# A two-block model on one core: where weight slabs are split around a sublayer change, and in which halves the second token tile is transposed

## The chip, the cores and the metric

The program runs on one core of one Trainium2 chip, as one launch. The metric is device microseconds of an execution, from the first to the last instruction of the core and the little that lies around it. Before the change three runs gave 1186.57, 1189.31 and 1192.03 us; the median is 1189.31 us.

## The reference

Two networks run one behind the other on a sequence of 256 tokens and a model width of 1024, all in float32.

```python
# first block: DEPTH = 2 layers
h = h + merge_heads(mix) @ w_o[layer]                 # MoBA attention, then forgetting attention
h = h + squared_relu_mlp(rms_norm(h, mlp_norm[layer]), w_up[layer], w_down[layer])   # D_FF = 4096
...
return rms_norm(h, final_norm)

# second block: nine vectors sh, sc, g from a condition c
h = modulate(rmsnorm(x, norm_ffn1[l]), sh1, sc1)
x = x + 0.5 * g1[:, None, :] * swiglu(h, ffn1_w_gate[l], ffn1_w_up[l], ffn1_w_down[l])   # width 2816
h = modulate(rmsnorm(x, norm_mix[l]), sh2, sc2)
x = x + g2[:, None, :] * hybrid_mixer(h, ...)         # state space and latent attention
h = modulate(rmsnorm(x, norm_ffn2[l]), sh3, sc3)
x = x + 0.5 * g3[:, None, :] * swiglu(h, ffn2_w_gate[l], ffn2_w_up[l], ffn2_w_down[l])
return rmsnorm(x, norm_final)
```

`swiglu(h)` is `(silu(h @ w_gate) * (h @ w_up)) @ w_down`. Here the second MLP of the first block is called M1, the first SwiGLU F1, the hybrid mixer X, and the second SwiGLU F2. The change touches the three borders M1 to F1, F1 to X, and X to F2.

## The kernel before, in words

Every product is made of three matmuls in a fast format: each operand is split into a high part and a low part, and high·high, high·low and low·high are added up in PSUM. The splits are the main work of the other engines. For a weight slab (256 rows by 512 columns, 512 KB) one DMA on SP's queue fills a tile `raw`; ScalarE (ACT) casts it into `wh` (line 179, or 183 with a gain), and VectorE (DVE) subtracts to get `wl` (line 180 or 184). There are five buffers for `raw` and five for `wh` and `wl` together, so a load is issued when the slab five places earlier has been split.

The tokens are two tiles, `t` = 0 and 1, of 128 tokens each. The normalised activations are transposed by TensorE (PE, line 272, four 128x128 transposes for a half of the 1024 features), cast by ACT into `xh` (line 266) and split by DVE into `xl` (line 267). These transposed tiles `xT` have four buffers of the kind "x".

A list `plan` holds all slabs in the order in which they are loaded and split. `take(i)` gives the product that needs slab `i` its parts, and it also splits up to two later slabs ahead, in the order of the list. Loads of the modulation weights (`w_ada`) are mixed into the list; four of them end in a cross-partition sum on POOL (line 509). Two kinds of slabs do not use the five buffers: *early* slabs, the first 768 rows of the next sublayer's first weight, have buffers of their own (`qh`, `ql`, lines 169 and 170); *spare* slabs, the second column half of the last but one down product, use the "x" buffers of the `xT` that the last up product reads, so they can only be split when that product is through with them.

A sublayer with a hidden layer goes cut by cut: the up product (F1 and F2: gate and up products) of cut j, then the down product of cut j-1. The up products take weights as the stationary side and 256 tokens as columns (lines 252 to 254); the down products and the first products of a sublayer take token blocks as the stationary side (lines 219 to 221, 512 columns). In the list, the early slabs of the next sublayer stand behind the last up product, just ahead of the last down slabs (`following`, in `plan_hidden`).

At the end of a sublayer the order is by token tile: column halves 0 and 1 of tile 0, then the spare half's products for tile 1, then tile 1. Each finished piece is added to `h` by DVE and starts a piece of the next norm. Such side chains are Python generators that a counter advances between products (`tick`, `yield n`), and `finish` runs one to its end. The normed tile goes through `modulated`, which writes `hn` (line 1029) and then transposes both halves. For tile 1, `finish(chains[1])` ahead of tile 1's first product runs both halves in one go, so PE gets eight transposes, ACT two casts and DVE two splits in a row; behind them come the splits of the next weight slabs.

Engines run their instructions in order. The order is that of the written program; nothing reschedules it.

Of the kernel before, what the change touches and what calls it, by code (L numbers as in the profile page):

```python
# [28 lines left out]
def kernel(ctx: ExitStack, tc: tile.TileContext, a: dict, out: bass.AP):  # L29
# [42 lines left out]
    def tok(t):  # L72
        return slice(t * TP, (t + 1) * TP)
# [42 lines left out]
    hold = []  # L116
    midway, second = [], []
    on_pool = set()

# [71 lines left out]
    def take(i):  # L191

        load_ahead()
        more = 0 if hold else 2 if i else 1
        while at["prep"] < len(plan):
            e = plan[at["prep"]]
            if at["prep"] > i:
                own = e[0] is not None and (e[6] or e[7])
                if not more or not (own or at["live"] < WB):
                    break  # L200
                more -= e[0] is not None and not own
            prepare()
            load_ahead()
        return ready[i]
# [206 lines left out]
    def plan_hidden(ups, w_down, cuts, rate, after=0, ahead=None, following=None):  # L411

        up, down = [], []
        for j in range(len(cuts) + 1):
            mixed["rate"] = rate if after < j < len(cuts) - 1 else 0.0
            if j < len(cuts):
                c0, n = cuts[j]
                got = [slab(w, 0, 8, c0, n, g, m=2 if n == 512 else 4) if j + i or not ahead else
                       ahead + slab(w, 6 * TP, 2, c0, n, g) for i, (w, g) in enumerate(ups)]
                up.append(got)  # L420
            if j == len(cuts) and following is not None:
                following()
            if j > 0:
                c0, n = cuts[j - 1]
                down.append([slab(w_down, c0, n // TP, s * 512, 512,
                                  spare=following is not None and j == len(cuts) - 1 and s == 1) for s in range(2)])
        mixed.update(rate=0.0, due=0.0)
        return up, down
# [413 lines left out]
    def hidden(plans, cuts, up, update, order=None, tail=None):  # L842
# [5 lines left out]
        for j in range(len(cuts) + 1):  # L848
            new = up(j, ups[j]) if j < len(cuts) else None
            if j == 1:  # L850
                acc = [[acc_ps() for _ in range(2)] for _ in range(2)]
# [173 lines left out]

    def modulated(xT, t, src, ys, r, shift):

        for s in range(2):
            DVE.scalar_tensor_tensor(out=ys[s], in0=src[s], scalar=r, in1=shift[:, cols(s)], op0=OP.mult, op1=OP.add)

        yield 8 if t else 4
        into_xT(xT, t, 0, blocks(ys[0]))
        yield 1
        into_xT(xT, t, 1, blocks(ys[1]))

# [5 lines left out]
    def norm_chain(shift, gain):  # L1041

        xT, ss, ys, chains = [], [None, None], [[], []], [None, None]

        def part(t, s):
# [6 lines left out]
            if s == 1:  # L1052
                yield 1
                r = rsqrt(total(ss[t], 2, EPS))
                yield from modulated(xT, t, ys[t], ys[t], r, shift)

# [4 lines left out]
    def two_norms_chain(fin, shift, gain):  # L1061

        xT, ss, su, u, chains = [], [None, None], [None, None], [[], []], [None, None]

        def part(t, s):
# [8 lines left out]
            if s == 1:  # L1074
# [5 lines left out]
                rr, r = rsqrt(w), rsqrt(v)  # L1080
                yield from modulated(xT, t, halves(h[t]), [sb("rb", name="hn") for _ in range(2)], rr, shift)
                start(residual(t, r))
# [10 lines left out]
    def ready_tokens(chains):  # L1093

        def before(t, k):
            finish(chains[t])
            if t == 1:
                hold.clear()
        return before

# [76 lines left out]
    def mixer(xT, chains, gate, next_chain, between):  # L1177
# [304 lines left out]
        acc = [[acc_ps() for _ in range(2)] for _ in range(2)]  # L1482
        finish(*norms)
        for n in range(3):
            if n == 1:
# [166 lines left out]
```

## Time and profile before

| what | value |
|---|---|
| median of 3 runs | 1189.31 us (1186.57 to 1192.03) |
| profiled execution, its own time | 1188.71 us |
| its span, first to last instruction | 1187.0 us |
| mean granted clock of TensorE | 0.996 of full speed |
| PE busy | 1162.7 us, 98% of the span |
| DVE busy | 832.5 us, 70% |
| ACT busy | 673.9 us, 57% |
| POOL busy | 250.8 us, 21% |
| DMA | 243.04 MB, mean 205 GB/s |

The profiled execution lies 0.6 us under the median of the three runs. The span is cut into 40 slices on the page: PE is at nine tenths or more in nearly all of them. Matmuls are pipelined, so one is shown as 0.39 us long while the next starts 0.23 us behind it; the pace is read from start to start. An idle time in brackets at the end of a row is what the engine waited just before that instruction, and behind the arrow stands what ended the wait. M1 ends and F1 begins near 600 us of the span, F1 ends and X begins near 800 us, X ends and F2 begins near 995 us.

### The profile page before, as it was taken

What the parts mean: (1) busy time and instruction counts of PE and PEld (TensorE: products, weight loads), DVE (VectorE), ACT (ScalarE), POOL (GpSimd) and SP (SyncE); (2) the same over time, 40 slices, a digit from 0 to 9 for tenths busy, and PEclk for the clock granted to TensorE, in tenths of its full rate; (3) what the DMA queues carried; (4) which work ended last, traced back from release to release, by engine and by line L of the source; (5) the groups of instructions that cost most, each with busy time, mean ns of one, the idle gap of its engine ahead of it and who ended that gap; (6) DMA issues with size and microseconds to landing.
All of it is one profiled execution on the core that took longest, in us unless ns stands there. A gap on an engine that the chain in (4) does not pass through costs nothing. (4 is left out here: it accounts for less than half of the span.)

```text
span 1187.0 us, 19943 instructions
## 1 busy us (share of the span) xinstructions
PE 1162.7 (98%) x7669; PEld 1047.6 (88%) x7669; DVE 832.5 (70%) x1187; ACT 673.9 (57%) x1148; POOL 250.8 (21%) x226
## 2 busy tenths in 40 slices
PE   8999999999999999999999999999998999999997
PEld 7987989988898799899878999978987887999996
DVE  5664678886666467788687788766776786766445
ACT  6476675565556675566654444535766573444443
POOL 3044202223003502112002121103147400112001
PEclk9999999999999999999999999999999999999999
DMA  8643567887553348799737978843733273777661
GB/s 270 195 142 107 181 219 262 295 287 223 170 174 123 129 151 282 242 308 318 244 133 256 314 274 303 275 154 101 222 92 107 90 268 125 244 222 246 209 193 38
DMA packets 128479, 243.04 MB, mean 205 GB/s; under 512 B 8515, under 2 KB 16612, under 8 KB 128384
## 3 DMA queue, kind: packets, MB, share of 16 engines
q1 hardware_dynamic: 126688, 239.96, 61.4%
q0 software_dynamic: 1376, 1.28, 0.5%
q8 instruction: 60, 0.98, 0.3%
q10 hardware_dynamic: 320, 0.53, 0.1%
q14 instruction: 35, 0.29, 0.1%
HBM read 240.65 MB, written 1.09 MB: 204 GB/s over the span
## 5 line engine op out<-in xcount | busy, mean ns | idle before, releaser
L179 ACT CAST wh<-raw 128x1024 fp32r<-128x1024 f32 (+1 forms) x231 | 237.4, 1041 | 220.3 <-DMA raw<-in_w_down_dram 64.1
L180 DVE TENSOR_TENSOR wl<-raw,wh 128x1024 fp32r<-128x1024 f32 (+1 forms) x201 | 261.5, 1319 | 128.0 <-ACT wh L179 125.9
L252 PE MATMUL mm<-xh,wh 128*128 128x256 f32 x1088 | 308.5, 284 | 0.0
L254 PE MATMUL mm<-xh,wl 128*128 128x256 f32 x1088 | 307.9, 283 | 0.0
L253 PE MATMUL mm<-xl,wh 128*128 128x256 f32 x1088 | 307.9, 283 | 0.0
L184 DVE SCALAR_TENSOR_TENSOR wl<-raw,cols,wh 128x512 fp32r<-128x512 f32 (+1 forms) x270 | 203.8, 806 | 65.2 <-ACT wh L183 65.1
L219 PE MATMUL acc<-wh,mh 128*128 128x512 f32 x524 | 208.0, 397 | 2.4 <-ACT mh L266 2.4
L183 ACT ACTIVATE wh<-raw,cols 128x512 fp32r<-128x512 f32 (+1 forms) x270 | 176.0, 708 | 59.3 <-PE acc L253 20.1
L253 PEld LDWEIGHTS mm<-xl,wh 128*128 128x128 f32 x1088 | 208.8, 192 | 0.8
L252 PEld LDWEIGHTS mm<-xh,wh 128*128 128x128 f32 x1088 | 208.8, 192 | 0.8
L254 PEld LDWEIGHTS mm<-xh,wl 128*128 128x128 f32 x1088 | 208.7, 192 | 0.0
L221 PE MATMUL acc<-wh,ml 128*128 128x512 f32 x524 | 205.1, 391 | 0.0
L220 PE MATMUL acc<-wl,mh 128*128 128x512 f32 x524 | 204.9, 391 | 0.0
L509 POOL PARTITION_ALL_REDUCE ada<-ada x18 | 64.3, 3572 | 338.2 <-DVE ada L504 140.2
L219 PEld LDWEIGHTS acc<-wh,mh 128*128 128x128 f32 x524 | 98.9, 189 | 24.4 <-ACT mh L266 4.0
L221 PEld LDWEIGHTS acc<-wh,ml 128*128 128x128 f32 x524 | 98.6, 188 | 22.5 <-DVE ml L267 1.5
L220 PEld LDWEIGHTS acc<-wl,mh 128*128 128x128 f32 x524 | 99.0, 189 | 19.1 <-DVE wl L180 0.5
L504 DVE SCALAR_TENSOR_TENSOR ada<-raw,c_act,ada 128x512 f32<-128x512 f32 x144 | 107.8, 748 | 3.5 <-DMA raw<-in_w_ada_dram 1.0
L252 PE MATMUL acc<-xh,wh 128*128 128x256 f32 x352 | 102.0, 290 | 0.0
L253 PE MATMUL acc<-xl,wh 128*128 128x256 f32 x352 | 99.5, 283 | 0.0
L254 PE MATMUL acc<-xh,wl 128*128 128x256 f32 x352 | 99.5, 283 | 0.0
L180 POOL TENSOR_TENSOR wl<-raw,wh 128x1024 fp32r<-128x1024 f32 x30 | 71.8, 2396 | 108.9 <-ACT wh L179 103.7
(320 smaller groups left out, 1602.4 us busy)
## 6 DMA issues: line engine op xcount, KB each, us to landing
raw<-in_w_ada_dram SPq DMA_DIRECT2D x72, 512.0 KB, 5.4
raw<-in_w_up_dram SPq DMA_DIRECT2D x64, 512.0 KB, 4.8
raw<-in_w_down_dram SPq DMA_DIRECT2D x64, 512.0 KB, 5.6
raw<-in_ffn_w_gate_dram SPq DMA_DIRECT2D x44, 512.0 KB, 4.9
raw<-in_ffn_w_up_dram SPq DMA_DIRECT2D x44, 512.0 KB, 4.8
raw<-in_ffn_w_down_dram SPq DMA_DIRECT2D x44, 512.0 KB, 4.8
raw<-in_moba_w_qkv_dram SPq DMA_DIRECT2D x23, 512.0 KB, 5.8
raw<-in_w_in_dram SPq DMA_DIRECT2D x20, 512.0 KB, 4.4
```

The costliest lines, as they stand in the source:

```text
L179: ACT.copy(hi, raw)
L180: (POOL if i in on_pool else DVE).tensor_tensor(lo, raw, f(hi), op=OP.subtract)
L183: ACT.mul(hi[:, k], raw[:, k], gain[k])
L184: DVE.scalar_tensor_tensor(out=lo[:, k], in0=raw[:, k], scalar=gain[k], in1=f(hi[:, k]), op0=OP.mult, op1=OP.subtract)
L219: PE.matmul(p, lhsT=xh, rhs=wh, start=first and n == 0, stop=False)
L220: PE.matmul(p, lhsT=xh, rhs=wl, start=False, stop=False)
L221: PE.matmul(p, lhsT=xl, rhs=wh, start=False, stop=last and n == len(ws) - 1)
L252: PE.matmul(o, lhsT=wh[:, c], rhs=xh, start=k == 0 and n % 2 == 0, stop=False)
L253: PE.matmul(o, lhsT=wh[:, c], rhs=xl, start=False, stop=False)
L254: PE.matmul(o, lhsT=wl[:, c], rhs=xh, start=False, stop=k == 7 and n % 2 == 1)
L504: DVE.scalar_tensor_tensor(out=acc, in0=raw[:, i, :], scalar=c_act[:, k:k + 1], in1=acc, op0=OP.mult, op1=OP.add)
L509: POOL.partition_all_reduce(acc, acc, TP, ReduceOp.add)
```

## The change

Three things change. In `plan_hidden`, the early slabs of the next sublayer now stand ahead of the last up product's slabs instead of behind it. `take` no longer splits a spare slab ahead of time before `spare["free"]` is set, which happens once the last up product and its hidden part have been written. In `modulated`, tile 1's halves become two chains that `ready_tokens` finishes one by one, the second only ahead of the fifth block of 128 features; tile 0's second half is split into its cast and, one `tick` later, its subtraction. `k // 4` is 0 for the first four blocks of 128 features and 1 for the rest.

```diff
--- before.py
+++ after.py
@@ -115,6 +115,7 @@
     mixed = {"rate": 0.0, "due": 0.0}
     hold = []
     midway, second = [], []
+    spare = {"free": False}
     on_pool = set()
 
     def slab(w, r0, nk, c0, n, gain=None, m=None, early=0, spare=False):
@@ -196,7 +197,7 @@
             e = plan[at["prep"]]
             if at["prep"] > i:
                 own = e[0] is not None and (e[6] or e[7])
-                if not more or not (own or at["live"] < WB):
+                if not more or not (own or at["live"] < WB) or (e[0] is not None and e[7] and not spare["free"]):
                     break
                 more -= e[0] is not None and not own
             prepare()
@@ -413,13 +414,13 @@
         up, down = [], []
         for j in range(len(cuts) + 1):
             mixed["rate"] = rate if after < j < len(cuts) - 1 else 0.0
+            if j == len(cuts) - 1 and following is not None:
+                following()
             if j < len(cuts):
                 c0, n = cuts[j]
                 got = [slab(w, 0, 8, c0, n, g, m=2 if n == 512 else 4) if j + i or not ahead else
                        ahead + slab(w, 6 * TP, 2, c0, n, g) for i, (w, g) in enumerate(ups)]
                 up.append(got)
-            if j == len(cuts) and following is not None:
-                following()
             if j > 0:
                 c0, n = cuts[j - 1]
                 down.append([slab(w_down, c0, n // TP, s * 512, 512,
@@ -847,6 +848,8 @@
         ups, downs = plans
         for j in range(len(cuts) + 1):
             new = up(j, ups[j]) if j < len(cuts) else None
+
+            spare["free"] = j == len(cuts) - 1
             if j == 1:
                 acc = [[acc_ps() for _ in range(2)] for _ in range(2)]
             if 0 < j < len(cuts):
@@ -1023,15 +1026,28 @@
         ACT.activation(out=a_bc, in_=a_bc, func=AF.Exp)
 
 
-    def modulated(xT, t, src, ys, r, shift):
+    def modulated(xT, t, src, ys, r, shift, parts):
 
         for s in range(2):
             DVE.scalar_tensor_tensor(out=ys[s], in0=src[s], scalar=r, in1=shift[:, cols(s)], op0=OP.mult, op1=OP.add)
-
-        yield 8 if t else 4
-        into_xT(xT, t, 0, blocks(ys[0]))
-        yield 1
-        into_xT(xT, t, 1, blocks(ys[1]))
+        if t == 0:
+            yield 4
+            into_xT(xT, t, 0, blocks(ys[0]))
+            yield 1
+
+            hi, lo = (x[:, :, tok(t)] for x in xT[1])
+            p = mm_ps((TP, 4, TP))
+            for j, b in enumerate(blocks(ys[1])):
+                PE.transpose(p[:, j, :], b, ident)
+            ACT.copy(hi, p)
+            yield 1
+            DVE.tensor_tensor(lo, p, f(hi), op=OP.subtract)
+            return
+
+        def half(s):
+            yield 1000
+            into_xT(xT, t, s, blocks(ys[s]))
+        parts += [start(half(s)) for s in range(2)]
 
     def add_gated(acc, t, c, gate):
         y = sb("ra", (TP, c.stop - c.start), name="gated")
@@ -1040,7 +1056,7 @@
 
     def norm_chain(shift, gain):
 
-        xT, ss, ys, chains = [], [None, None], [[], []], [None, None]
+        xT, ss, ys, chains = [], [None, None], [[], []], [None, None, []]
 
         def part(t, s):
             if s == 0:
@@ -1052,7 +1068,7 @@
             if s == 1:
                 yield 1
                 r = rsqrt(total(ss[t], 2, EPS))
-                yield from modulated(xT, t, ys[t], ys[t], r, shift)
+                yield from modulated(xT, t, ys[t], ys[t], r, shift, chains[2])
 
         def go(t, s):
             chains[t] = start(part(t, s))
@@ -1060,7 +1076,7 @@
 
     def two_norms_chain(fin, shift, gain):
 
-        xT, ss, su, u, chains = [], [None, None], [None, None], [[], []], [None, None]
+        xT, ss, su, u, chains = [], [None, None], [None, None], [[], []], [None, None, []]
 
         def part(t, s):
             if s == 0:
@@ -1078,7 +1094,8 @@
                 DVE.tensor_tensor(w, su[t][:, 0:1], su[t][:, 1:2], op=OP.add)
                 DVE.scalar_tensor_tensor(out=w, in0=v, scalar=EPS, in1=w, op0=OP.mult, op1=OP.add)
                 rr, r = rsqrt(w), rsqrt(v)
-                yield from modulated(xT, t, halves(h[t]), [sb("rb", name="hn") for _ in range(2)], rr, shift)
+                yield from modulated(xT, t, halves(h[t]), [sb("rb", name="hn") for _ in range(2)], rr, shift,
+                                     chains[2])
                 start(residual(t, r))
 
         def residual(t, r):
@@ -1096,6 +1113,8 @@
             finish(chains[t])
             if t == 1:
                 hold.clear()
+
+                finish(chains[2][k // 4])
         return before
 
     def ffn(plans, xT, chains, gate, next_chain, between, tail=None):
@@ -1481,6 +1500,7 @@
 
         acc = [[acc_ps() for _ in range(2)] for _ in range(2)]
         finish(*norms)
+        spare["free"] = True
         for n in range(3):
             if n == 1:
                 between()
```

The first place is DVE's order around the last gate product of F1. Before:

```order
L1150 TENSOR_TENSOR gu<-sg,mm 128x512
L267 TENSOR_TENSOR ml<-gu,mh 128x512
L1150 TENSOR_TENSOR gu<-sg,mm 128x512
L267 TENSOR_TENSOR ml<-gu,mh 128x512
L504 SCALAR_TENSOR_TENSOR ada<-raw,c_act,ada 128x512 x2
L180 TENSOR_TENSOR wl<-raw,wh 128x1024 x12
L170 TENSOR_TENSOR ql<-raw,qh 128x400 x6
L180 TENSOR_TENSOR wl<-raw,wh 128x1024 x2
L1150 TENSOR_TENSOR gu<-sg,mm 128x512
L267 TENSOR_TENSOR ml<-gu,mh 128x512
L1150 TENSOR_TENSOR gu<-sg,mm 128x512
L267 TENSOR_TENSOR ml<-gu,mh 128x512
```

Now (line 170 has become 171, 180 has become 181, 1150 is 1169):

```order
L1169 TENSOR_TENSOR gu<-sg,mm 128x512
L268 TENSOR_TENSOR ml<-gu,mh 128x512
L1169 TENSOR_TENSOR gu<-sg,mm 128x512
L268 TENSOR_TENSOR ml<-gu,mh 128x512
L505 SCALAR_TENSOR_TENSOR ada<-raw,c_act,ada 128x512 x2
L171 TENSOR_TENSOR ql<-raw,qh 128x400 x6
L181 TENSOR_TENSOR wl<-raw,wh 128x1024 x10
L1169 TENSOR_TENSOR gu<-sg,mm 128x512
L268 TENSOR_TENSOR ml<-gu,mh 128x512
L1169 TENSOR_TENSOR gu<-sg,mm 128x512
L268 TENSOR_TENSOR ml<-gu,mh 128x512
```

`ql` is the low part of an early slab of X, `ada` a step of the modulation, `wl` the low part of a weight slab. The six `ql` have moved from behind twelve `wl` to ahead of the first; the first `wl` of the row of ten belongs to the first slab of the last gate product. Six `wl` (two of them spare) now stand behind the hidden part (`gu`, `ml`) where two stood.

The second place is ACT's order at the same kind of border in M1, around the last up product. Before:

```order
L179 CAST wh<-raw 128x1024 x4
L886 ACTIVATE relu<-mm 128x512
L888 ACTIVATE sq<-relu 128x512
L266 CAST mh<-sq 128x512
L886 ACTIVATE relu<-mm 128x512
L888 ACTIVATE sq<-relu 128x512
L266 CAST mh<-sq 128x512
L183 ACTIVATE wh<-raw,cols_122 128x512 x8
L179 CAST wh<-raw 128x1024 x4
L169 CAST qh<-raw 128x512 x6
L179 CAST wh<-raw 128x1024 x2
```

Now (line 169 has become 170, 183 has become 184, 266 is 267, 886 is 889):

```order
L180 CAST wh<-raw 128x1024 x4
L170 CAST qh<-raw 128x512 x6
L889 ACTIVATE relu<-mm 128x512
L891 ACTIVATE sq<-relu 128x512
L267 CAST mh<-sq 128x512
L889 ACTIVATE relu<-mm 128x512
L891 ACTIVATE sq<-relu 128x512
L267 CAST mh<-sq 128x512
L184 ACTIVATE wh<-raw,cols_122 128x512 x8
L180 CAST wh<-raw 128x1024 x2
```

`qh` is the high part of an early slab of F1; `relu`, `sq` and `mh` evacuate an up product, and the eight `wh` with `cols` are the slabs of the last up product. The six `qh` now stand ahead of the evacuation of the last but one up product, and two of four plain `wh` have moved away behind the next evacuation.

The third place is DVE's order when M1 gives over to F1. Before:

```order
L267 TENSOR_TENSOR xl<-mm,xh 128x4x128 x2
L893 SCALAR_TENSOR_TENSOR h_103<-acc,r_5017,h_103 128x512
L1069 TENSOR_TENSOR u<-h_103,fin 128x512
L1073 TENSOR_TENSOR h_103<-u,mod 128x512
L1087 TENSOR_SCALAR h_102<-u,y 128x512 x2
L1077 TENSOR_SCALAR v<-ss 128x1
L1078 TENSOR_TENSOR w<-su 128x1
L1079 SCALAR_TENSOR_TENSOR w<-v,w 128x1
L1029 SCALAR_TENSOR_TENSOR hn<-h_103,y,mod 128x512 x2
L267 TENSOR_TENSOR xl<-mm,xh 128x4x128 x2
L180 TENSOR_TENSOR wl<-raw,wh 128x1024 x4
```

Now (line 893 has become 896 and stands just ahead of the first row shown, 1087 is 1104, 1029 is 1032):

```order
L1044 TENSOR_TENSOR xl<-mm,xh 128x4x128
L1085 TENSOR_TENSOR u<-h_103,fin 128x512
L1089 TENSOR_TENSOR h_103<-u,mod 128x512
L1093 TENSOR_SCALAR v<-ss 128x1
L1094 TENSOR_TENSOR w<-su 128x1
L1095 SCALAR_TENSOR_TENSOR w<-v,w 128x1
L1032 SCALAR_TENSOR_TENSOR hn<-h_103,y,mod 128x512 x2
L1104 TENSOR_SCALAR h_102<-u,y 128x512 x2
L1104 TENSOR_SCALAR h_103<-u,y 128x512 x2
L268 TENSOR_TENSOR xl<-mm,xh 128x4x128
L181 TENSOR_TENSOR wl<-raw,wh 128x1024 x4
L268 TENSOR_TENSOR xl<-mm,xh 128x4x128
```

Line 893 is the last sum of tile 1 into `h`, `hn` the modulated norm, line 1087 a scaling of the residual that only the end of F1 reads. The last sum now stands ahead of the second `xl` of tile 0. Of tile 1's two `xl`, the first now stands behind four scalings, of which two stood ahead of the norm and two behind the `wl` before, and the second stands behind the four `wl`. At the other two borders it is the same without the scalings. ACT has the same order there: one `xh`, four `wh`, one `xh`.

## Rows read from the trace of the kernel before

**Rows 1.** The page, busy time of each engine, share of the span, instructions.
```profile
PE 1162.7 (98%) x7669; PEld 1047.6 (88%) x7669; DVE 832.5 (70%) x1187; ACT 673.9 (57%) x1148; POOL 250.8 (21%) x226
```

**Rows 2.** Waits of PE, whole span: us in total, times, longest us.
```profile
PE acc L219 <- ACT mh L266: 2.4, 2, 1.6
...
PE mm L272 <- DVE hn L1029: 1.4, 2, 1.1
```

**Rows 3.** Timeline of PE, ends of M1 and F1: start us, us, instruction, idle before.
```profile
591.50 0.39 PE L221 MATMUL acc<-wh,ml 128*128 128x512 f32 x1
...
597.00 0.39 PE L221 MATMUL acc<-wh,ml 128*128 128x512 f32 x1
...
605.86 0.39 PE L221 MATMUL acc<-wh,ml 128*128 128x512 f32 x1
...
783.48 0.39 PE L221 MATMUL acc<-wh,ml 128*128 128x512 f32 x1
...
790.86 0.40 PE L221 MATMUL acc<-wh,ml 128*128 128x512 f32 x1
```

**Rows 4.** Stretches: length, busy time by engine, granted clock (PEclk), DMA share, GB/s.
```profile
787.20:790.60 3.40, 3.40 (x8) 2.44 (x8) 2.89 (x3) 2.88 (x4) 0.00 (x0) 0.50 0.09 31
811.10:814.50 3.40, 3.40 (x11) 3.40 (x11) 3.01 (x5) 1.79 (x4) 0.00 (x0) 0.50 0.33 84
```

**Rows 5.** Timeline of ACT, end of F1.
```profile
775.59 1.05 ACT L179 CAST wh<-raw 128x1024 fp32r<-128x1024 f32 x1 [4.71 <-PE mm L253]
...
781.89 1.05 ACT L179 CAST wh<-raw 128x1024 fp32r<-128x1024 f32 x1 [1.72 <-DMA raw<-in_ffn_w_down_dram]
```

**Rows 6.** Timelines of DVE, POOL and PE around F1's last gate product.
```profile
750.24 1.22 DVE L180 TENSOR_TENSOR wl<-raw,wh 128x1024 fp32r<-128x1024 f32 x1
751.38 3.26 DVE L180 TENSOR_TENSOR wl<-raw,wh 128x1024 fp32r<-128x1024 f32 x1
...
777.82 3.00 DVE L170 TENSOR_TENSOR ql<-raw,qh 128x400 fp32r<-128x400 f32 x6
...
750.51 4.05 POOL L509 PARTITION_ALL_REDUCE ada<-ada  x1 [19.97 <-ACT wh L179]
...
752.48 0.28 PE L252 MATMUL mm<-xh,wh 128*128 128x256 f32 x1
```

**Rows 7.** Timelines of SP, ACT, DVE and PE around M1's last up product.
```profile
561.62 1.53 SPq L149 DMA_DIRECT2D raw<-in_w_up_dram  x2
...
563.53 0.59 ACT L886 ACTIVATE relu<-mm 128x512 f32<-128x512 f32 x1
...
567.90 5.39 DVE L184 SCALAR_TENSOR_TENSOR wl<-raw,cols,wh 128x512 fp32r<-128x512 f32 x8
...
572.03 0.28 PE L252 MATMUL mm<-xh,wh 128*128 128x256 f32 x1
```

**Rows 8.** Chain that ended last: a load at F1's end by itself.
```profile
777.93 3.89 DMA raw<-in_ffn_w_down_dram
```

**Rows 9.** DMA issues from 543 to 587 us: count, size, median us to landing.
```profile
raw<-in_w_down_dram SPq DMA_DIRECT2D x10, 512.0 KB, 5.8
```

**Rows 10.** Timeline of DVE, M1 giving over to F1.
```profile
611.99 0.88 DVE L1087 TENSOR_SCALAR h<-u,y 128x512 f32<-128x512 f32 x2
...
613.91 1.42 DVE L1029 SCALAR_TENSOR_TENSOR hn<-h,y,mod 128x512 f32<-128x512 f32 x2 [0.66 <-POOL y L324]
616.10 1.35 DVE L267 TENSOR_TENSOR xl<-mm,xh 128x512 fp32r<-128x512 f32 x2 [0.77 <-ACT xh L266]
617.70 4.63 DVE L180 TENSOR_TENSOR wl<-raw,wh 128x1024 fp32r<-128x1024 f32 x4 [0.26 <-ACT wh L179]
```

**Rows 11.** Timelines of DVE and PE, F1 giving over to X.
```profile
803.07 0.69 DVE L267 TENSOR_TENSOR xl<-mm,xh 128x512 fp32r<-128x512 f32 x1 [0.81 <-ACT xh L266]
...
811.36 2.76 DVE L180 TENSOR_TENSOR wl<-raw,wh 128x576 fp32r<-128x576 f32 x4
...
810.17 0.45 PE L219 MATMUL acc<-qh,xh 128*128 128x400 f32 x1 [1.00 <-ACT xh L266]
```

## The prediction

> **What bounds the kernel now.** I read the busy times first: PE is busy for 98% of the span, and the next engine, DVE, for 70% [rows 1]. So a gain can only come out of PE's few gaps, and each new gap is paid in full. The waits of PE come second. Those that this change can reach are two waits for the hidden part's cast, 2.4 us together, the longer 1.6, and two for tile 1's normed halves, 1.4 us [rows 2]. Third comes the timeline, for what a gap costs beyond its own length. In the quiet stretch at M1's end 39 matmuls of 512 columns start in 8.86 us, 0.227 us each. Fifteen starts at the end of M1 take 5.50 us where 15 x 0.227 = 3.41 would do, so 2.1 us are lost; at the end of F1 fifteen take 7.38, so 4.0 are lost [rows 3]. The rest of the 4.0 is the clock: 3.4 us at half of it, the lower of its two levels, follow F1's gap, and 3.4 us more follow the gaps at F1's border with X [rows 4]. A fall of the clock thus costs 3.4/2 = 1.7 us. Fourth, what ends the gap at F1's end: ACT's cast of the second spare slab stands in line until the last matmul of the up product has read `xT` (4.71 us of waiting, to 775.59), and the load that the five full buffers held back arrives at 781.89 [rows 5]. The hidden part stands behind both.
>
> **The change part by part.** The sum is made against the profiled execution's own 1188.71 us.
>
> *Ends of M1 and F1, a gain.* With the early slabs done and the spare splits behind the hidden part, nothing stands between the last up product and `mh`. In F1 the evacuation takes about 3 us after the product, and PE has 24 x 0.227 = 5.4 us of down products before it needs anything new. The last down loads sit in the buffers by then, because the early slabs gave theirs back. DVE then makes one split per 1.16 us (a quarter of 4.63 [rows 10]), while PE uses one per 6 matmuls or 1.36 us at the tightest place. I take both losses as gone: -2.1 and -4.0. Bounds: at the least half of each, if one split is late; no more than all.
>
> *F1's last gate product, a loss.* What the early slabs left behind they now meet here: six `ql` on DVE stand ahead of the first `wl` of that product. Before, this `wl` began at 750.24 and ended at 751.46, and the product began at 752.48; its third matmul, 0.24 later at 752.72, is the first that needs `wl` [rows 6]. The cover is 1.3 us. The six `ql` take 3.00 us. And the same place has the cross-partition sum on POOL, from 750.51 on: the split that met it took 3.26 us where the one ahead of it took 1.22, so 2.04 more [rows 6]. Either a `ql` or the `wl` meets it now. So the `wl` ends at 750.24 + 3.00 + 2.04 + 1.22 = 756.5, and PE waits 3.8 us. That gap is longer than the 1.6 us that preceded a fall of the clock, so I add 1.7: +5.5. Bounds: +1.7 (3.00 less the 1.3 of cover, no stretch, no fall) and +6.5 (one more `wl` late).
>
> The Trainium skill, page "SBUF — State Buffer", section "Who interferes with whom", says that a DVE instruction with two SBUF inputs contends with a GpSimd instruction that reads SBUF, and that the one that comes first keeps the shared ports for its whole length. The stretched `wl` has two such inputs, and so have all six `ql`. The trace agrees on the stretch, 3.26 beside 1.22. By the rule as it stands a `ql` would wait for the whole 3.2 us that a sum lasts once it has the ports, not for 2.04, and the term would be +6.7; I keep the row's number.
>
> *M1's last up product, a small loss.* Here the `qh` stand on ACT ahead of the evacuation of the product before. They take over SP's issue places of the first three up slabs; the third of these is 561.62 + 1.16 = 562.78 [rows 7]. A load by itself lands after 3.89 us [rows 8], at 566.7; two casts of half a slab (0.53 each, half of 1.05 [rows 5]) end at 567.7. The `relu` that began at 563.53 begins 4.2 us later. The first split of the up product ended at 567.90 + 0.67 (an eighth of 5.39) = 568.57 and now ends at 572.8; PE needs it two matmuls after 572.03, at 572.3 [rows 7]. So +0.5. Bounds: 0, and +2.4 if the load takes the 5.8 us that loads take on this busy queue [rows 9].
>
> *Tile 1 of the three borders, a loss twice.* Before, both `xl` of tile 1 were made ahead of four weight splits. Now PE has 12 matmuls with the first half, then the transposes of the second, and that half's `xl` stands behind four `wl`. From the first `xl` to the second DVE needs 4.63 + 0.68 = 5.3 us [rows 10]; PE has, after the two matmuls that need no `xl`, 10 x 0.227, four transposes at about 0.35, and two matmuls more, 3.1 in all. It waits 2.2, and the second transposes, which a wait covered before, show for 0.35: +2.6. This holds for M1 to F1 and for X to F2. At M1 to F1 the last sum comes 0.68 earlier (half of 1.35), so `hn`, which ended at 615.33, ends at 614.65; but four scalings at 0.44 now stand ahead of the first `xl`, which begins at 616.4 where it began at 616.10 [rows 10]: +0.3. So +2.9 and +2.6. Bounds for each: +1 (ACT and DVE half hidden) and +4.6 with a fall of the clock.
>
> *F1 to X.* The last sum stood behind an `xl` that waited 0.81 us and took 0.69; it is 1.5 us earlier, and so is the product that began at 810.17 [rows 11]. Its weights are narrower: four `wl` take 2.76, with the `xl` 3.4 us, against 12 x 0.18 (400 of 512 columns of 0.227) + 0.35 = 2.5 of PE's, so 0.9 of waiting and 0.35 of transposes come in. That is -0.2 with the fall of the clock after 811 kept [rows 4], and -1.9 without it. I take -1.2, nearer to the second, as the gaps become shorter.
>
> *Nothing for the rest.* The number of loads, splits, matmuls and transposes is the same; POOL's order does not change.
>
> **Sum.** -2.1 - 4.0 + 5.5 + 0.5 + 2.9 + 2.6 - 1.2 = +4.2 us, so 1192.9 us against the profiled execution. That one lies 0.6 under the median of its three runs; I put 1193.2.
>
> **The rivals.**
>
> *A. The clock falls at the new gaps of tile 1 too.* M1 to F1 and X to F2 get gaps of about 1 us on either side of two matmuls. For it: at F1 to X two waits of 1.1 and 1.0 us with eight transposes between them preceded a fall [rows 2, 4, 11]. Against it: M1's end had a wait of 0.8 (2.4 less 1.6) and no fall [rows 2]. Each fall adds 1.7: one gives 1194.9, both 1196.6, which is slower by 0.6%. It decides when PE stands still about as long in sum as at F1 to X.
>
> *B. Only the gains come.* If DVE reaches the six `ql` before the hidden part keeps it busy, and the second `xl` are ready in time, only -2.1 - 4.0 - 1.9 is left: 1180.7. For it speaks that DVE has 30% free over the span [rows 1]. Against it speaks the order on DVE and ACT, which they cannot leave; it needs the splits to run twice as fast as their rows.
>
> *C. The sum on POOL keeps DVE out for its whole length,* as the rule of the skill has it: +1.2 on the gate term, 1194.4. For it: the sum's 4.05 us [rows 6]. Against it: the split's 3.26 in the same rows.
>
> **How the numbers follow.** About 0.5%, 5.9 us, is what a measurement of this kernel can tell from no change: slower begins at 1195.3, faster ends at 1183.4. My forecast, that gains and new waits nearly cancel, gets 0.58; its own terms are good to some 2.5 us, so I give 0.46 to no change and 0.12 to slower. A gets 0.26: 0.10 of it within, 0.16 slower. B gets 0.08, of which 0.07 faster and 0.01 within. C gets 0.08: 0.05 within, 0.03 slower. That makes 0.07 faster, 0.62 the same, 0.31 slower. The range runs from 1187.0 (gate term at its lower bound, the rest as summed, less 2 us of spread of the runs) to 1198.5 (A with both falls and 2 us more). What is left out is B and the upper ends of several terms together.
>
> **What the profile of the changed kernel would show.** PE's waits for `mh` at the ends of M1 and F1 gone, and no half clock after F1's up product. A wait of PE for a `wl` of some 3.8 us at the start of F1's last gate product, DVE's six `ql` just ahead of it with one of them or the first `wl` stretched to 2.5 us or more, and half clock behind. Waits of PE for `xh` and `xl` of 2 us in the middle of tile 1's first product, at M1 to F1 and X to F2, with four `wl` on DVE right ahead of that `xl`. ACT's `relu` of M1's last but one up product some 4 us later against PE. I am wrong if the gate product starts without a wait, if tile 1's second half is split in time, or if the time falls under 1187.

## The result and the profile after

The changed kernel takes 1196.60 us (median of 4 runs, 1195.45 to 1200.87), the kernel before 1187.94 beside it (median of 4, 1186.30 to 1192.03): a ratio of 1.0082, 95% interval 1.0064 to 1.0099. It is slower by 0.8%. The range held the time, but the likeliest case, no change that can be measured, did not come. The profiled execution took 1195.72 us with a span of 1194.0, against 1188.71 and 1187.0, so the two traces differ by 7.0 us and show most of the 8.7 of the medians.

I compared when the same matmul starts in both traces, stage by stage: each step of that difference is a gain or a loss in its place.

| place | predicted | trace |
|---|---|---|
| M1's last up product | +0.5 | +0.9 |
| M1's end | -2.1 | -2.1 |
| M1 to F1 | +2.9 | +3.1 |
| F1's last gate product | +5.5 | +5.8 |
| F1's end | -4.0 | -4.0 |
| F1 to X | -1.2 | +0.4 |
| X to F2 | +2.6 | +3.2 |

That is +7.3, less 0.3 of drift ahead of the first of these places. PE's own work is the same; its waits are others.

The page's busy times, which answer to [rows 1], and below them PE's waits over the whole span, which answer to [rows 2]:

```profile
PE 1162.9 (97%) x7669; PEld 1048.9 (88%) x7669; DVE 831.3 (70%) x1187; ACT 673.8 (56%) x1148; POOL 248.6 (21%) x226
```

```profile
PE mm L255 <- DVE wl L181: 4.1, 1, 4.1
PE mm L220 <- ACT xh L267: 3.5, 5, 0.8
PE acc L220 <- ACT xh L267: 3.5, 4, 1.6
PE mm L222 <- DVE xl L268: 2.1, 2, 1.1
```

The two waits for `mh` are gone, and one of 4.1 us for a weight split stands at the top, followed by tile 1's `xh` and `xl`. The timeline of PE at the ends of M1 and F1 answers to [rows 3]:

```profile
592.11 0.39 PE L222 MATMUL acc<-wh,ml 128*128 128x512 f32 x1
...
595.51 0.39 PE L222 MATMUL acc<-wh,ml 128*128 128x512 f32 x1
...
604.35 0.39 PE L222 MATMUL acc<-wh,ml 128*128 128x512 f32 x1
...
790.88 0.39 PE L222 MATMUL acc<-wh,ml 128*128 128x512 f32 x1
...
794.28 0.39 PE L222 MATMUL acc<-wh,ml 128*128 128x512 f32 x1
```

Fifteen starts take 3.40 us at both ends, where they took 5.50 and 7.38. ACT shows why at F1's end [rows 5]: the casts of `mh` come first now, and the spare slabs' casts behind them, with no load to wait for.

```profile
783.12 0.62 ACT L267 CAST mh<-gu 128x512 fp32r<-128x512 f32 x1 [7.54 <-DVE gu L1169]
785.10 0.62 ACT L267 CAST mh<-gu 128x512 fp32r<-128x512 f32 x1 [1.35 <-DVE gu L1169]
785.62 4.85 ACT L180 CAST wh<-raw 128x1024 fp32r<-128x1024 f32 x5
```

F1's last gate product (DVE, POOL, PE) answers to [rows 6]:

```profile
752.30 5.04 DVE L171 TENSOR_TENSOR ql<-raw,qh 128x400 fp32r<-128x400 f32 x6
...
752.79 2.61 DVE L171 TENSOR_TENSOR ql<-raw,qh 128x400 fp32r<-128x400 f32 x1
...
757.26 2.35 DVE L181 TENSOR_TENSOR wl<-raw,wh 128x1024 fp32r<-128x1024 f32 x2
752.57 3.40 POOL L510 PARTITION_ALL_REDUCE ada<-ada  x1 [19.41 <-ACT qh L170]
754.05 0.28 PE L253 MATMUL mm<-xh,wh 128*128 128x256 f32 x1
758.53 0.39 PE L255 MATMUL mm<-xh,wl 128*128 128x256 f32 x1 [4.09 <-DVE wl L181]
```

The six `ql` (the first row) take 5.04, which is 3.00 and the 2.04 that the sum on POOL adds; the first `wl` starts only then. The whole stretch lies on the second of the six (the row of 2.61); the other five take 0.56 to 0.57 each. The stretches at half clock (length, busy time by engine, granted clock) answer to [rows 4]; the last two are tile 1's at the borders into F1 and F2:

```profile
758.90:762.30 3.40, 3.40 (x19) 3.40 (x18) 2.49 (x3) 2.42 (x3) 0.00 (x0) 0.51 1.02 375
813.30:816.70 3.40, 3.40 (x14) 3.25 (x12) 2.23 (x4) 1.13 (x2) 0.00 (x0) 0.51 0.59 180
613.50:622.10 8.60, 6.09 (x27) 4.12 (x26) 7.36 (x10) 5.45 (x7) 0.00 (x0) 1.00 0.41 126
1000.80:1009.50 8.70, 6.16 (x28) 4.14 (x27) 5.92 (x6) 5.45 (x7) 0.00 (x0) 1.00 0.43 129
```

The fall after F1's up product is gone, one behind the gate product has come, and the one at F1 to X has stayed. M1's last up product (ACT, DVE, PE) answers to [rows 7]: `relu` starts at 567.57 instead of 563.53, and PE waits 0.28 for the first split.

```profile
567.57 0.59 ACT L889 ACTIVATE relu<-mm 128x512 f32<-128x512 f32 x1
571.94 5.39 DVE L185 SCALAR_TENSOR_TENSOR wl<-raw,cols,wh 128x512 fp32r<-128x512 f32 x8
572.75 0.39 PE L255 MATMUL mm<-xh,wl 128*128 128x256 f32 x1 [0.28 <-DVE wl L185]
```

M1 giving over to F1, DVE and then PE, answers to [rows 10]:

```profile
614.94 0.68 DVE L268 TENSOR_TENSOR xl<-mm,xh 128x512 fp32r<-128x512 f32 x1
615.81 4.63 DVE L181 TENSOR_TENSOR wl<-raw,wh 128x1024 fp32r<-128x1024 f32 x4 [0.19 <-ACT wh L180]
620.36 0.69 DVE L268 TENSOR_TENSOR xl<-mm,xh 128x512 fp32r<-128x512 f32 x1
614.89 0.50 PE L220 MATMUL mm<-qh,xh 128*128 128x512 f32 x1 [0.78 <-ACT xh L267]
618.10 0.60 PE L273 MATMUL mm<-ident,hn 128*128 128x128 f32 x4
619.38 0.50 PE L220 MATMUL mm<-qh,xh 128*128 128x512 f32 x1 [0.68 <-ACT xh L267]
621.10 0.50 PE L222 MATMUL mm<-qh,xl 128*128 128x512 f32 x1 [0.99 <-DVE xl L268]
```

The second `xl` stands 4.63 us behind, as forecast, and PE stops at tile 1's first product, in its middle for `xh` and once more for `xl`. F1 giving over to X, PE, then ACT, then one row of DVE, answers to [rows 11]:

```profile
809.96 0.60 PE L273 MATMUL mm<-ident,hn 128*128 128x128 f32 x4
812.19 0.45 PE L220 MATMUL acc<-qh,xh 128*128 128x400 f32 x1 [1.64 <-ACT xh L267]
816.03 0.99 PE L273 MATMUL mm<-ident,hn 128*128 128x128 f32 x4
817.69 0.45 PE L220 MATMUL acc<-qh,xh 128*128 128x400 f32 x1 [0.67 <-ACT xh L267]
810.54 0.48 ACT L1239 COPY cq<-acc 128x384 f32<-128x384 f32 x1 [2.76 <-DVE dtr L1237]
811.05 0.52 ACT L306 ACTIVATE junk<-cq 128x384 f32<-128x384 f32 x1
811.57 0.56 ACT L267 CAST xh<-mm 128x512 fp32r<-128x512 f32 x1
...
817.66 0.69 DVE L268 TENSOR_TENSOR xl<-mm,xh 128x512 fp32r<-128x512 f32 x1 [2.13 <-ACT xh L267]
```

ACT does `cq`'s copy and square ahead of the cast, so that with four transposes in place of eight PE stands still for 1.64 where it stood for 1.00; the clock falls, and the second four transposes take 0.99 for 0.60. DVE has its four `wl` done and waits 2.13 for the second `xh`, and PE does not wait for that `xl`.

### The profile page after: what moved, and what is told of

Same layout as the page of the kernel before. It is cut to its first block, busy times and chain, and to the rows that moved or that the text cites. A ratio compares the mean times of both kernels' runs of the same rounds, so it can differ in the third digit from the quotient of the medians.

```text
span 1194.0 us, 19939 instructions
## 1 busy us (share of the span) xinstructions
PE 1162.9 (97%) x7669; PEld 1048.9 (88%) x7669; DVE 831.3 (70%) x1187; ACT 673.8 (56%) x1148; POOL 248.6 (21%) x226
```

## The experiments

The theory, T1: three parts with prices of their own. The early down slabs give 6.1 us at the two ends and take it back at F1's last gate product; tile 1's halves one by one cost at every border; the first tile's split is small. The rivals: the early slabs' loads cost all over (R1), or the transposes one by one cost whatever DVE does (R2). All of these ran beside the kernel before, whose median was 1187.3 to 1187.4 us.

| run | early slabs | tile 1's halves | first tile split | us | ratio, 95% interval |
|---|---|---|---|---|---|
| e1 | as after | together | no | 1188.43 | 1.0008, 0.9999 to 1.0016 |
| e2 | as before | one by one | yes | 1196.09 | 1.0069, 1.0057 to 1.0081 |
| e3 | as before, spare rule kept | together | no | 1193.94 | 1.0052, 1.0040 to 1.0063 |
| e4 | M1: as after; F1: behind the gate product | together | no | 1181.57 | 0.9951, 0.9939 to 0.9963 |
| e5 | as after | one by one, splits held back | yes | 1192.11 | 1.0040, 1.0026 to 1.0053 |
| e6 | as after, one sum left out | one by one | yes | 1190.59 | 1.0031, 1.0019 to 1.0044 |
| e8 | M1: middle of the last up product; F1: as e4 | together | no | 1183.18 | 0.9960, 0.9947 to 0.9972 |
| e9 | as e8 | together | yes | 1179.72 | 0.9934, 0.9922 to 0.9945 |
| e10 | as e4 | together | yes | 1180.54 | 0.9941, 0.9927 to 0.9955 |
| e11 | as e4 | one by one | yes | 1190.73 | 1.0027, 1.0015 to 1.0040 |
| e12 | as e4 | one by one, splits held back | yes | 1186.35 | 0.9993, 0.9984 to 1.0002 |
| e13 | as before | together | yes | 1186.21 | 0.9988, 0.9979 to 0.9997 |

**e1 and e2, either part alone.** e1 takes `modulated` back from the changed kernel:

```diff
-            hi, lo = (x[:, :, tok(t)] for x in xT[1])
...
+            into_xT(xT, t, 1, blocks(ys[1]))
...
-        parts += [start(half(s)) for s in range(2)]
+        yield 8
+        into_xT(xT, t, 0, blocks(ys[0]))
+        yield 1
+        into_xT(xT, t, 1, blocks(ys[1]))
...
-                finish(chains[2][k // 4])
```

e2 takes the place of the early slabs back, and the spare rule:

```diff
-                if not more or not (own or at["live"] < WB) or (e[0] is not None and e[7] and not spare["free"]):
+                if not more or not (own or at["live"] < WB):
...
-            if j == len(cuts) - 1 and following is not None:
-                following()
...
+            if j == len(cuts) and following is not None:
+                following()
```

> This run undoes the change of the second tile's halves (the first tile's last sums go back too) and keeps the early down slabs ahead of the last up product. Theory T1 (engines take their work in order, and the time is the sum of what each border gives or takes): the first MLP's last up product +0.9 us, its end -2.1, the second MLP's last gate product +5.85 (4.1 of waiting for the weight split behind six early splits, the rest at half clock), its end -4.0, the three borders as before. Sum +0.6 us, about 1188.5, against 1187.9 before and 1196.6 after. Rival R1 (the early slabs cost by their transfers: raw buffers and queues are taken earlier everywhere, so the loss is spread over the kernel): well above that, 1191 or more, with longer waits for DMA in the last slabs. Rival R2 (the loss is the halves one by one alone, and the early slabs are a gain without a price): 1184 or less.

> This run does the other part alone: the early down slabs behind the last up product as before, the second tile's halves one by one and the first tile's last sums between the casts as after. T1: first to second sublayer +3.1 us (a little less, as ACT's squares come earlier to the end of the first MLP, which waits for mh as before), second MLP to the cross sublayer +0.4, cross sublayer to the last MLP +3.3; both ends and both last products as before. Sum +6 to +7, about 1194.5, so that the part without this one is worth less than 1 us. Rival R1 (the early slabs carry most of the loss): 1190 or less.

e1 came out at +1.1 us and e2 at +8.8, which together is the +8.7 of the change to about 1 us. So the halves carry the loss, R1 falls in both, and so does R2 of e1, for which it would have been 1184 or less. In e1's trace the ends give -2.1 and -4.0 and the gate product takes +4.1. There the wait is shorter than in the changed kernel, since DVE begins the six `ql` 3.5 us ahead of the product and not 1.75:

```profile
748.20 5.04 DVE L171 TENSOR_TENSOR ql<-raw,qh 128x400 fp32r<-128x400 f32 x6
...
751.68 0.28 PE L253 MATMUL mm<-xh,wh 128*128 128x256 f32 x1
...
754.43 0.42 PE L255 MATMUL mm<-xh,wl 128*128 128x256 f32 x1 [2.35 <-DVE wl L181]
```

e2 costs 1.6 us more than T1 had it. Its profiled execution, 1193.71, is the fastest of five: the trace shows +2.4 at M1 to F1, +0.5 at F1 to X, +3.1 at X to F2, and -1.0 at F1's end, where the fall of the clock is missing, +5.0 in all. The other 3.8 of the +8.8 have no place in it.

**e5, the four splits held back until the second half is done.**

```diff
             if t == 1:
-                hold.clear()
-
                 finish(chains[2][k // 4])
+                if k >= 4:
+                    hold.clear()
```

> The changed kernel, but the four weight splits that go to DVE between the two lower halves of tile 1 are held back until the second half is done, so that on DVE both lower halves stand in a row, and the four splits behind them. T1 (the loss at the two borders into an MLP is the second lower half's place behind 4.63 us of splits): the wait of 1.0 to 1.1 for xl at both borders goes, and the two up groups start earlier; about 2.2 us back at each of the two borders and up to 0.9 at the third, about 1191.5 against 1196.6. Rival R2 (the loss is the transposes one by one themselves, two waits of 0.7 to 0.8 for ACT's copies at each border, whatever DVE does): 1195 to 1197, with the waits for xh unchanged. Rival R3 (the splits held back are then missed by the products that follow): the wait moves to wl by about as much, 1195 to 1197 too, but in the waits for the weight splits.

4.5 us came back of the 5 expected (3.9, if each is taken against the kernel before that ran beside it). The wait for `xl` is gone, the waits for `xh` are not, as R2 had it; in the traces the borders into F1 and F2 give back 1.2 and 1.7, not 2.2 each. R3 does not show at the borders: no wait for a weight split stands there. At the gate product that wait is 4.3 where it was 4.1, and a new one of 1.2 for a `wh` comes ahead of it. The profiled execution, 1196.88, was the slowest of the twelve: its two falls of the clock last 6.8 us each.

**e6, one sum on POOL less.**

```diff
-            POOL.partition_all_reduce(acc, acc, TP, ReduceOp.add)
+            if n != 15:
+                POOL.partition_all_reduce(acc, acc, TP, ReduceOp.add)
```

> The changed kernel without the one cross-partition sum that GpSimd runs beside the six early splits at the second MLP's last gate product (the second half of one modulation row is thereby not summed over the partitions; everything else is computed). T1: the six splits are stretched by that sum from 3.00 to 5.04 us, so without it they take 3.0, the wait of 4.1 at the gate product falls to about 2.0, and the time by 2.0, or by up to 3.7 if the half clock behind the wait goes with it: 1193 to 1194.6 against 1196.6. Rival R1 (the wait is for late weight transfers, and the splits only stand there): the wait stays at 4.1 and the time at 1196.6. Rival C of the prediction (the splits stand still for the sum's whole 3.40): the six take 1.64 or less.

The six take 3.00 and the wait is 1.74, as T1 has it (DVE, then PE):

```profile
751.41 3.00 DVE L171 TENSOR_TENSOR ql<-raw,qh 128x400 fp32r<-128x400 f32 x6
...
755.59 0.39 PE L255 MATMUL mm<-xh,wl 128*128 128x256 f32 x1 [1.74 <-DVE wl L181]
```

The sum's share is therefore 2.04 of stretch, not its whole length. The gate term falls from +5.8 to +3.5. The time fell by 6.0 (5.4 in the same way), more than that: in this trace F1 to X has no fall of the clock and stands at -1.2, 1.6 less. Of the other 2 us 0.6 are at X to F2 and 0.6 in small steps at three other places; the rest has no place in the profile.

**e4 and e8, the early slabs elsewhere.** In e4 F1's early slabs go between the last gate and the last up product:

```diff
+                for i, (w, g) in enumerate(ups):
+                    if j == len(cuts) - 1 and following is not None and i == 1:
+                        following()
+                    got.append(slab(w, 0, 8, c0, n, g, m=2 if n == 512 else 4) if j + i or not ahead else
```

In e8 M1's early slabs also go behind the first half of its last up product's weights (in F1 they stand as in e4, but the last gate and up weights are loaded in pieces of two):

```diff
+                    got = [slab(w, 0, 4, c0, n, None if g is None else g[:4], m=2)]
+                    if len(ups) == 1:
+                        following()
+                    got[0] += slab(w, 4 * TP, 4, c0, n, None if g is None else g[4:], m=2)
```

> Halves as before, as in the first run of this study, but in the second MLP the early down slabs stand between the last gate product and the last up product, so that on DVE the gate product's four weight splits come ahead of the six early ones. T1 (the gate product waits because its splits stand behind the six; 2.35 us of waiting and 1.7 of half clock in the first run, 1188.4): the gate term of +4.1 goes, the end of the MLP keeps its -4.0, and the six splits fit between the gate's and the up's (the gate product lasts 11.5 us): 1188.4 - 4.1 = 1184.3, against 1187.3 before. Rival R1 (the six splits hold up whatever comes next): the wait moves to the last up product and the time stays at 1187 to 1188.5. Rival R2 (the clock falls anyway at that place): 1186.

> As the run before it, and in the first MLP too the early down slabs are moved into the middle of the last up product (behind the first half of its weights). T1: the +0.1 to +0.9 that the first MLP's last up product paid goes: 1183.5 to 1184.2. Rival: what is split in the middle of a product is missed by its second half, +1: 1185.3.

e4 gained 5.8 us: the gate product's four splits come first and the six behind them, and nothing waits (DVE, then PE).

```profile
746.14 6.67 DVE L181 TENSOR_TENSOR wl<-raw,wh 128x1024 fp32r<-128x1024 f32 x4
752.74 2.99 DVE L171 TENSOR_TENSOR ql<-raw,qh 128x400 fp32r<-128x400 f32 x6
...
750.58 0.28 PE L255 MATMUL mm<-xh,wl 128*128 128x256 f32 x1
```

It beat its forecast by 2.7. In the traces F1 to X, which had no fall either, accounts for 1.2 of that (-1.6 where e1 has -0.4) and X to F2 for 0.8. M1's middle place is worth nothing: M1's last up product costs 0.0 in e4's trace as in e8's. e8 is 1.6 slower, and its trace has the fall at F1 to X that e4's lacks.

**e9, e10 and e13, the first tile's second half.** To e8, to e4 and to the kernel before, the split of the first tile is added, and nothing else:

```diff
-            into_xT(xT, t, 1, blocks(ys[1]))
...
+                PE.transpose(p[:, j, :], b, ident)
+            ACT.copy(hi, p)
+            yield 1
+            DVE.tensor_tensor(lo, p, f(hi), op=OP.subtract)
```

> As the run before it, with the first tile's second half split as in the changed kernel (its four transposes and ACT's cast first, the last sums between, then DVE's subtraction), tile 1's halves together as before. T1 (the last sums start earlier on DVE, and with them tile 1's squares and transposes; 0.4 us earlier in the trace of the changed kernel at the first border): -0.4 at each border into an MLP, up to -0.8 in all, 1183. Rival (the first tile's products then wait for the later subtraction): +0.6 at each, 1185.

> The early down slabs behind the last gate product in the second MLP and ahead of the last up product in the first (as in the run at 1181.6 us), and the first tile's second half split with the last sums between; tile 1's halves together as before. T1 (that split lets DVE do the last sums while ACT casts, so that tile 1's transposes find their input; the middle place in the first MLP is worth nothing): 1179.7, as the run at 1179.7. Rival (the split was worth it only together with the middle place): 1181.6.

> The kernel before with one part of the change alone: the first tile's second half split, the last sums between the cast and the subtraction. T1 (worth 1.9 us, the difference of the runs at 1181.6 and 1179.7, wherever the early slabs stand): 1185.4. Rival (the split pays only where the ends of the MLPs are early): 1187.3.

It gained 3.5, 1.0 and 1.1 us. Only the 3.5 is well clear of the noise: the intervals of e4 and e10 overlap, and that of e13 ends at 0.9997. A worth of 1.9 wherever the early slabs stand, as T1 of e13 had it, does not show; e10's 1180.5 lies between its T1 and the rival; in e9 the gain is over four times the 0.8 of T1, and its rival falls. PE shows it in e10 at F1 to X: the wait of 1.1 for `hn` ahead of tile 1's transposes [rows 2] is gone. In the traces F1 to X takes 2.9, 0.8 and 2.9 less than without the split. In the first and the last of these 1.7 is a fall of the clock that is missing, which leaves 0.8 to 1.2 for the split; whether it also prevents the fall is not shown, as e3 and e4 have none without it.

```profile
800.86 1.29 PE L273 MATMUL mm<-ident,hn 128*128 128x128 f32 x8
803.14 0.45 PE L220 MATMUL acc<-qh,xh 128*128 128x400 f32 x1 [1.00 <-ACT xh L267]
```

**e11 and e12, the halves with nothing else in the way.** The changed kernel with e4's place, and with e5's edit besides.

> The changed kernel with one thing moved: in the second MLP the early down slabs stand behind the last gate product. Tile 1's halves go one by one with the four weight splits between them, as in the changed kernel. T1 (the halves cost +2.5 and +2.6 to 3.3 at the borders into an MLP, the gate term of 5.9 is gone, and so is what the late DVE added there): 1196.6 less some 8, 1188 to 1189. Rival (the gate wait is only moved to the last up product): 1192 or more.

> As the run before it, with the four weight splits held back until tile 1's second half is done. T1 (both the splits between the two lower halves and the transposes one by one cost): 1.2 and 1.8 back at the two borders, 1185 to 1186. R2 (only the transposes one by one cost): as the run before it, 1188 to 1189. R4 (only the splits between cost): 1179.7 to 1181.6, as with the halves together.

Beside e10 they isolate the halves: e12 is 5.8 us slower, the price of the transposes one by one; e11 4.4 more, the price of four `wl` between the two `xl`. So neither R2 nor R4 alone. The three borders of the traces show 4.4 of the 5.8 and 2.6 of the 4.4. Some 2.3 of the 4.4 may be clock: e11's executions have a mean granted clock of 0.9965, e12's 0.9984, as e10's (0.0019 x 1190, an estimate). e11 itself is 1.7 slower than T1 had it; its rival falls, as no wait stands at F1's last gate or up product. In e12 (DVE, then PE) both `xl` stand ahead of the splits, but the second cannot start before the second transposes, and PE stops twice for `xh` of tile 1 where e10 stops once, for 0.35:

```profile
617.40 0.69 DVE L268 TENSOR_TENSOR xl<-mm,xh 128x512 fp32r<-128x512 f32 x1
621.82 0.69 DVE L268 TENSOR_TENSOR xl<-mm,xh 128x512 fp32r<-128x512 f32 x1 [3.73 <-ACT xh L267]
617.34 0.50 PE L220 MATMUL mm<-qh,xh 128*128 128x512 f32 x1 [0.78 <-ACT xh L267]
620.56 0.60 PE L273 MATMUL mm<-ident,hn 128*128 128x128 f32 x4
621.84 0.50 PE L220 MATMUL mm<-qh,xh 128*128 128x512 f32 x1 [0.67 <-ACT xh L267]
```

**e3, the spare rule without the early slabs' new place.** e1, with the second of e2's edits.

> Halves as before and the early slabs at their old place behind the last up product; of the first part of the change only the rule is kept by which spare slabs are prepared not before the last cut. T1 (an end is late because ACT's and DVE's last hidden part stands behind the early slabs' casts and splits): by the order of instructions the rule alone lets the last hidden part stand ahead of the six early splits, so that most of -2.1 and -4.0 stays, and no gate product waits for them: 1181 to 1184. Rival (the weights of the last down slabs, which now share the stretch with the early ones, arrive late): the ends wait for wl in place of mh, 1187 to 1190.

T1 fell, and its rival was short by 4 us: the waits for `mh` go, and PE waits 7.6 us for the last down slabs' weights, whose loads ACT waits for (PE's waits over the span, then ACT at M1's end).

```profile
PE acc L220 <- ACT wh L180: 4.1, 3, 2.2
PE acc L221 <- DVE wl L181: 3.5, 5, 0.8
...
592.57 1.04 ACT L180 CAST wh<-raw 128x1024 fp32r<-128x1024 f32 x1 [1.25 <-DMA raw<-in_w_down_dram]
```

## Why the prediction was partly wrong

*Ends of M1 and F1.* Right to 0.1 us, here and in every run that has the early slabs ahead of the last up product or in it.

*M1's last up product.* +0.9 for +0.5. With the same order at this place e1, e4 and e11 have 0.0, e5 and e6 0.9 and 0.7, and e12 3.5 with a fall of the clock, so that this order alone does not fix the size.

*F1's last gate product.* Right in its parts: 3.8 of waiting forecast, 4.09 measured, and one fall of the clock behind it. The 0.3 comes with a later DVE: it starts on the six 1.75 us ahead of the product, where I had 2.24 [rows 6]. e6 showed the stretch to be 2.04 and e4 that the order alone causes the wait. By the rule of the Trainium skill, page "SBUF — State Buffer", section "Who interferes with whom", a `ql` would have been kept out until the sum ends; six would take some 6.1 (an estimate: 3.00 and the 3.10 that is left of the sum's 3.40 when the first `ql` has ended). The measured 5.04, against 3.00 in e6, decides for the contention and against that length: the one `ql` that was kept out ended 0.6 ahead of the sum. Rival C did not happen.

*M1 to F1 and X to F2.* Right in the mechanism and short by 0.2 and 0.6. In the middle of tile 1's first product the traces have +2.8 at both borders for my 2.6. The rest at X to F2 is tile 0's first product, which starts 0.5 late. At M1 to F1 it starts 0.6 late too, behind a wait for `xh`: M1's last matmul is 1.5 earlier (604.35 for 605.86), ACT's squares ahead of the cast only 0.9. There it did not make the sum worse: tile 1's first product starts 0.3 late against M1's end, as forecast; `hn` was ready at 613.45, just as PE came to tile 1's transposes at 613.50.

*F1 to X, the step that failed.* I put it at -1.2, "nearer to the second, as the gaps become shorter". The trace has +0.4. One gap became longer, 1.64 for 1.00, as ACT's cast stands behind `cq`'s copy and square whatever PE does, and the fall of the clock stayed. That is 1.0 of the miss of 1.6; the other 0.6 is against my -0.2 with the fall kept. The earlier start is right (1.4 for 1.5), but the 0.9 of waiting for an `xl` behind four `wl` did not come: PE waited 0.67 for the second `xh` instead, and with its transposes that costs 1.7, not 1.25. In e6 and e11, whose profiled executions have no fall there, the same order gives -1.2, where I had -1.9 (e12, with the splits held back, has none either, and -0.8). So the term hangs in part on the fall, and the fall did not hang on the halves: with them together it is in the traces of before, e1 and e8 and in none of e3, e4, e9, e10 and e13.

*Rival A.* The time is A's, 1196.6, but its mechanism is not: at tile 1's gaps into F1 and F2 the clock stays full. That its number came is chance. What the trace adds to my 4.2 is 1.6 at F1 to X, 0.6 at X to F2, 0.4 at M1's last up product, 0.3 at the gate and 0.2 at M1 to F1: 3.1, less the drift of 0.3, the difference between the trace's 7.0 and my 4.2. The 1.7 from there to the 8.7 of the medians belongs to no stage: the profiled execution before lies 0.8 over its median, the one after 0.9 under.

*The chances.* The change came out at 8.7 us for my 4.2. Six of seven terms were sound to 0.7 us, yet five of the errors went the same way. I called the sum good to 2.5 us as if the errors were independent; at the border terms they share a cause, PE stopping more often than in the rows that I had, and I let the clock fall at the gate in full and at F1 to X by less than half. The lower end of the range is 1187.4 by the terms that I gave for it, not 1187.0.

## What to carry to other kernels

On engines that work in order, a block of early work costs where it stands: count what of the next product it precedes, on each engine, and put it behind that product's own weights (e4 against e1: 6.9 us from the place alone, 4.1 of it at the gate product in the traces). Cutting one batch of transposes in two makes PE stop twice for the same round trip over ACT and DVE; here that cost 5.8 us, and filling the pause on DVE with other work 4.4 more, part of it perhaps clock. Of a change in three parts, time each alone: the smallest part here, the first tile's split, was the good one, though alone (e13) its gain is hardly clear of the noise, and with e8's or e4's order it makes a kernel of 1179.7 or 1180.5 us, faster than both.

## What the runs showed of the hardware beyond this

The granted clock differs from one execution of the same kernel to the next, and part of the time goes with it. Of the kernel before (beside e10 to e13) it was 0.998 in 17 of 29 executions and 0.995 in 3; in the changed kernel 0.993 to 0.995 in all four, in e10 0.998 or 0.999 in all five. By the means, 0.997 and 0.994, some 3.6 us of the 8.7 are clock (0.003 x 1190, an estimate). In e5 the executions at 0.998 and 0.993 are 10.5 us apart, at 1186.37 and 1196.88.

A sum over partitions on POOL stretched DVE's subtractions by 2.04 us both when one long split met it before, 3.26 for 1.22, and when six short ones do now, 5.04 for 3.00. Both times one subtraction bears all of it. The sum itself lasts 4.05 where 0.95 of the subtraction ahead was still to run when it began, and 3.40 where 0.30 was: 3.10 beyond that both times.
